# The transposed tokens of the two PEER stages moved by 64 bytes against the weights in on-chip memory

## The chip, the core and the metric

The kernel runs on one core of one Trainium2 chip. Time is device microseconds of one execution, from the median of a few runs. The core has a matrix engine (PE, whose weight loads are shown apart as PEld), a vector engine (DVE), a scalar engine (ACT), a further engine (POOL) and queues for transfers. SBUF is the on-chip memory of 128 partitions. A tile there is a byte range that is the same in every partition, and its address below is the first byte of this range.

## The reference

A trunk of two layers on 256 tokens of 1024 features: a token mixer (attention) in each layer, and after each one a PEER stage, which retrieves experts by product keys. Only the PEER stage is touched:

```python
q = (xc @ w_q).reshape(t, PEER_HEADS, 2, PEER_QDIM // 2)
sc = jnp.einsum('thpc,hpnc->thpn', q, sub_keys)
...                                        # top 16 of each half, then of their sums
u = u_tab[expert]
act = jax.nn.gelu(jnp.einsum('thkd,td->thk', u, xc), approximate=False)
w = (g * act).astype(xc.dtype)
return jnp.einsum('thk,thkd->td', w, v_tab[expert])
```

There are 16384 experts, and `u_tab` and `v_tab` are 16384 x 1024 in float32.

## The kernel before

No expert is gathered. A PEER stage (`peer`) multiplies all tokens with all experts and keeps the chosen ones by a gate matrix. It has three parts, each a long run of matmuls.

- The query projection: 16 blocks of `w_q`, each 8 chunks of 128 features, tokens as the moving operand (256 columns). Here the tokens are the tiles `rhi0..7` and `rlo0..7` of the pool `rawt`.
- The product with the up table: 128 blocks of 128 experts, tokens again the moving operand, now the normalised ones in `hi0..7` and `lo0..7` of the pool `hp`. Its result is `S`, which ScalarE takes through a GELU into `A`, while the gates are made beside it (`gates`, with its own small matmuls on L1011).
- The product with the down table: 128 blocks. The roles turn: the split activations (`ohA`, `ohB`, made by `wsplit` from `A`) are loaded as weights, and rows of the table are the moving operand (512 columns), summed in `acc`.

Every float32 operand is split into a high part of reduced width (`hi`) and the remainder (`lo`), and each product is three matmuls: high by high, and the two mixed ones. In the first two parts that is `split_prod` (L819 to L821): `a` and `b` are 128-column slices of a weight tile's high and low part, which PE loads, and `hi[c]`, `lo[c]` are token tiles of 128 x 256 in 4-byte elements, which PE streams. In the down table it is `mm` (L1099 to L1101).

All weights come through one class (`Weights`): a 512 KB transfer into `raw`, then for each half a ScalarE copy to `hi` (L69) and a VectorE subtraction to `lo` (L70), in five tiles each of 2048 bytes from the pools `hip` and `lop`. The slices loaded by `split_prod` are 512 bytes long.

Where the tiles lie (bytes; the number behind the slash is the address modulo 512, the residue): the weights' `hi` from 40096 / 160 and `lo` from 50336 / 160; `ident` at 24736 / 160; the tokens `hi0` at 172704 / 160, `rhi0` at 199328 / 160; `ohB` from 191136 / 160 and `ohA` from 195232 / 160. As all steps between tiles of a group are multiples of 512, each whole group has its first tile's residue. The filler tile of 192 bytes in `body` (pool `fill`) takes part in these numbers.

Three other places matter for the argument. The first projection (`product`, L301 to L303) has a group of 200-column matmuls in pairs: the second of a pair streams its weights from 800 bytes further on, so from residue 448, while the tokens that it loads stay at 160; the first streams from 160. The transposes of the attention (`transposed`, L400) load slices of the probabilities `P`, which lie at residue 0 in the first layer and at 448 in the second, and stream `ident` from 160 in both. The transposes of L713 load slices of `ks` and `qs` that are 384 bytes apart, so they run through four residues in turn, and stream `ident` too.

Of the kernel before, what the change touches and what calls it, by code (L numbers as in the profile page):

```python
# [9 lines left out]
F32 = mybir.dt.float32  # L10
# [136 lines left out]
def body(tc, I, out):  # L147
    nc = tc.nc
    with ExitStack() as ctx:
# [131 lines left out]
        def tiles8(pool, name, dtype=F32R):  # L281
            return [pool.tile([128, S], dtype, name=f"{name}{c}") for c in range(8)]
# [475 lines left out]
        def peer(layer, gcol, final=False):  # L758
            with ExitStack() as c1:
# [6 lines left out]
                def scr(n):  # L766
                    o = off[0]
                    off[0] += n
                    assert off[0] <= (NA - SCR) * S, off
                    return flat[:, o:o + n]  # L770

                hp = c1.enter_context(tc.tile_pool(name="hp", bufs=1))
# [3 lines left out]
                R1 = hp.tile([128, S // 4, 2, 4], BF, name="R1")  # L776
                RE, RM = hp.tile([128, S], BF, name="RE"), hp.tile([128, 2, S], F16, name="RM")
                RA = hp.tile([128, 3, 4 * len(GA)], F32, name="RA")
                hi, lo = tiles8(hp, "hi"), tiles8(hp, "lo")
                rawc = ExitStack()  # L780
                rawpool = rawc.enter_context(tc.tile_pool(name="rawt", bufs=1))
                scv = scr(2 * 16 * 128)
                sc = scv.rearrange("p (a b c) -> p a b c", a=2, b=16)
                sk = scr(2048).rearrange("p (j n) -> p j n", j=16)
# [82 lines left out]
                def stage2():  # L867
# [85 lines left out]
                    for k, (c, z) in enumerate(((r1T, 1.0), (e2, 1.0), (e2, -1.0))):  # L953
                        nc.scalar.activation(RA[:, k].rearrange("p (g t) -> p g t", t=4),
                                             c.rearrange("p (g t) -> p g t", t=4)[:, GA[0]::AM], AF.Copy, scale=z)
# [5 lines left out]
                def gates():  # L961
                    def hot(t0, E, G):
# [8 lines left out]
                        def pair(i, relu):  # L971
                            if act:
                                for j in (i, i + 1):
                                    r = [RA[:, n, k + j:k + j + 1] for n in range(3)]
                                    if relu:
# [140 lines left out]

        even_mixer(0)
        peer(0, 16)
        mla_mixer(8)
        peer(1, 24, True)  # L1120


# [59 lines left out]
```

## Time and profile before

| what | value |
| --- | --- |
| median of 3 runs | 1887.8 us (1887.28 to 1888.87) |
| the profiled execution | 1887.42 us, of which the span 1885.6 us and 1.8 us around it |
| PE | 1863.1 us busy, 99% of the span |
| PE weight loads | 1687.9 us, 90% |
| VectorE, ScalarE | 1433.7 us (76%), 1248.0 us (66%) |
| bytes read from HBM | 319.97 MB, 170 GB/s over the span |

The span is the time from the first to the last instruction of the profiled execution. Matmuls overlap in a pipeline: the duration of one is its latency, and the pace of the engine is the distance from one start to the next.

### The profile page before, as it was taken

Reading aid. Unit: us, or ns where it says so; the run is one execution under the profiler, and the core shown is the slowest. Engines: PE = TensorE matmul, PEld = TensorE weight load, DVE = VectorE, ACT = ScalarE, POOL = GpSimd, SP = SyncE. Lnnn points to the kernel's source line nnn. Section 1 sums busy time; section 2 is a strip of 40 time slices with the busy share of each in tenths; the row PEclk is TensorE's granted clock in tenths of the full one; section 3 lists DMA queues with packets and bytes.
Section 4 is the critical chain, followed back from the end, with each engine's and each line's share of the span. In section 5 each row is a group of like instructions: output and inputs, shape, how many; then the busy total and the mean of one; then the engine's idle time right before and its main releaser. Section 6 shows DMA issues by size and latency. Waiting matters only on the chain.

```text
span 1885.6 us, 35589 instructions
## 1 busy us (share of the span) xinstructions
PE 1863.1 (99%) x12568; PEld 1687.9 (90%) x12568; DVE 1433.7 (76%) x3586; ACT 1248.0 (66%) x3060; POOL 15.0 (1%) x34
## 2 busy tenths in 40 slices
PE   9999999999999999999999999999999999999998
PEld 7779999999999888888888899999999988888886
DVE  7968998878897666666677699987788976666665
ACT  5656557888876555555577565578888765555554
POOL 0000000000000000000000000000000000000000
PEclk9999999999999999999999999999999999999999
DMA  6434555555455665555553345555555555665664
GB/s 201 124 112 146 185 180 174 167 161 166 158 160 176 192 196 193 192 197 192 184 167 122 124 148 189 183 166 163 161 164 162 168 178 191 193 197 191 193 197 147
DMA packets 90178, 323.33 MB, mean 171 GB/s; under 512 B 10512, under 2 KB 10896, under 8 KB 89744
## 3 DMA queue, kind: packets, MB, share of 16 engines
q1 hardware_dynamic: 88416, 318.18, 52.9%
q8 instruction: 99, 1.62, 0.4%
q0 software_dynamic: 288, 2.10, 0.3%
q10 hardware_dynamic: 1296, 0.78, 0.1%
q14 instruction: 79, 0.65, 0.1%
HBM read 319.97 MB, written 1.05 MB: 170 GB/s over the span
## 4 chain that ended last, share of the span: by engine, by line
PE 95%; DVE 3%; ACT 1%; issue 0%; DMA 0%; POOL 0%; DVEq 0%; POOLq 0%; ACTq 0%
PE S L819 15%; PE S L820 15%; PE S L821 15%; PE acc L1099 12%; PE acc L1101 12%; PE acc L1100 12%; PE scp L1011 3%; PE pj L301 2%; PE pj L303 2%; PE pj L302 2%; DVE lo L70 1%; PE bk L375 1%; PE scp L1048 1%; PE pj L439 1%; PE pj L440 1%; PE pj L441 1%
## 5 line engine op out<-in xcount | busy, mean ns | idle before, releaser
L69 ACT ACTIVATE hi<-raw 128x512 fp32r<-128x512 f32 (+2 forms) x1214 | 756.2, 628 | 567.2 <-PE S L820 191.0
L70 DVE TENSOR_TENSOR lo<-raw,hi 128x512 fp32r<-128x512 f32 (+2 forms) x1214 | 825.8, 685 | 370.8 <-ACT hi L69 362.4
L819 PE MATMUL S<-hi,hi 128*128 128x256 f32 x2048 | 591.0, 289 | 0.5 <-ACT A L1040 0.5
L820 PE MATMUL S<-lo,hi 128*128 128x256 f32 x2048 | 580.6, 284 | 0.0
L821 PE MATMUL S<-hi,lo 128*128 128x256 f32 x2048 | 580.1, 284 | 0.0
L819 PEld LDWEIGHTS S<-hi,hi 128*128 128x128 f32 x2048 | 393.4, 192 | 0.9 <-ACT A L1040 0.9
L820 PEld LDWEIGHTS S<-lo,hi 128*128 128x128 f32 x2048 | 393.8, 192 | 0.0
L821 PEld LDWEIGHTS S<-hi,lo 128*128 128x128 f32 x2048 | 393.0, 192 | 0.0
L1100 PE MATMUL acc<-lo,ohB 128*128 128x512 f32 x512 | 199.5, 390 | 0.0
L1100 PE MATMUL acc<-lo,ohA 128*128 128x512 f32 x512 | 199.5, 390 | 0.0
L1101 PE MATMUL acc<-hi,ohA 128*128 128x512 f32 x512 | 199.2, 390 | 0.0
L1101 PE MATMUL acc<-hi,ohB 128*128 128x512 f32 x512 | 198.5, 390 | 0.0
L1099 PE MATMUL acc<-hi,ohB 128*128 128x512 f32 x512 | 158.5, 390 | 0.0
L1099 PE MATMUL acc<-hi,ohA 128*128 128x512 f32 x512 | 158.2, 390 | 0.0
L976 ACT ACTIVATE ohB<-ohB,RA 128x128 bf16<-128x128 bf16 x256 | 117.2, 525 | 0.0
L1099 PEld LDWEIGHTS acc<-hi,ohA 128*128 128x128 f32 x512 | 96.2, 188 | 19.9
L1100 PEld LDWEIGHTS acc<-lo,ohA 128*128 128x128 f32 x512 | 96.2, 188 | 19.9
L1101 PEld LDWEIGHTS acc<-hi,ohB 128*128 128x128 f32 x512 | 96.2, 188 | 19.9
L1101 PEld LDWEIGHTS acc<-hi,ohA 128*128 128x128 f32 x512 | 96.2, 188 | 19.8
L1099 PEld LDWEIGHTS acc<-hi,ohB 128*128 128x128 f32 x512 | 96.2, 188 | 19.8
L1100 PEld LDWEIGHTS acc<-lo,ohB 128*128 128x128 f32 x512 | 96.1, 188 | 19.9
L1040 ACT ACTIVATE A<-S 128x256 f32<-128x256 f32 (+43 forms) x252 | 76.0, 302 | 13.3 <-PE S L821 13.2
(261 smaller groups left out, 2428.9 us busy)
## 6 DMA issues: line engine op xcount, KB each, us to landing
raw<-in_pu SPq DMA_DIRECT2D x256, 512.0 KB, 3.5
raw<-in_pv SPq DMA_DIRECT2D x256, 512.0 KB, 4.3
raw<-in_pq SPq DMA_DIRECT2D x32, 512.0 KB, 3.5
raw<-in_w SPq DMA_DIRECT2D x20, 512.0 KB, 3.9
raw<-in_uq SPq DMA_DIRECT2D x9, 512.0 KB, 4.1
raw<-in_w SPq DMA_DIRECT2D x12, 352.0 KB, 3.0
raw<-in_w0o SPq DMA_DIRECT2D x8, 512.0 KB, 3.6
raw<-in_w1o SPq DMA_DIRECT2D x8, 512.0 KB, 3.5
```

Of the source, the lines that this page charges most:

```text
L69: self.nc.scalar.activation(hi[:, :w], src, AF.Copy)
L70: self.nc.vector.tensor_tensor(lo[:, :w], src, hi[:, :w].bitcast(F32), op=OP.subtract)
L301: nc.tensor.matmul(ps[tb], hi[c][:, t], a, start=st, stop=False)
L819: nc.tensor.matmul(p, a, hi[c], start=first and i == 0, stop=False)
L820: nc.tensor.matmul(p, a, lo[c], start=False, stop=False)
L821: nc.tensor.matmul(p, b, hi[c], start=False, stop=last and i == 3)
L976: nc.scalar.activation(e[:, j // 2, :, j % 2], e[:, j // 2, :, j % 2], AF.Relu, bias=r[1], scale=r[2])
L1011: nc.tensor.matmul(p[:, i], E[:, 1, i // 2, :, i % 2], G[:, s, i // 2, :, i % 2], start=i + s == 0, stop=True, skip_group_check=True)
L1040: nc.scalar.activation(a[:, T:], p[:, T:], AF.Gelu)
L1099: nc.tensor.matmul(o, a[:, 0, t], w[0], start=b == 0, stop=False)
L1100: nc.tensor.matmul(o, a[:, 0, t], w[1], start=False, stop=False)
L1101: nc.tensor.matmul(o, a[:, 1, t], w[0], start=False, stop=b == NK - 1)
```

## The change

Three tiles that nothing writes or reads are placed between others. `fill0` (448 bytes, that is 64 less than 512) ahead of the tokens `hi`, `lo`; `fill1` (64 bytes) behind them; `fill2` (448 bytes) ahead of `rhi`, `rlo`.

```diff
                 RA = hp.tile([128, 3, 4 * len(GA)], F32, name="RA")
+
+                hp.tile([128, 112], F32, name="fill0")
                 hi, lo = tiles8(hp, "hi"), tiles8(hp, "lo")
+                hp.tile([128, 16], F32, name="fill1")
                 rawc = ExitStack()
                 rawpool = rawc.enter_context(tc.tile_pool(name="rawt", bufs=1))
+                rawpool.tile([128, 112], F32, name="fill2")
```

The addresses that result:

| tiles | before | after |
| --- | --- | --- |
| weights `hi`, `lo`, `A`, `ident`, all of the mixers | unchanged | unchanged |
| tokens `hi0`.. | 172704 / 160 | 173152 / 96 |
| `act`, `ohB`, `ohA` | from 189088 / 160 | from 189600 / 160 |
| raw tokens `rhi0`.. | 199328 / 160 | 200288 / 96 |
| normalised `x` (`xn00`..) | 215712 / 160 | 216672 / 96 |
| `A1` | 199328 / 160 | 199840 / 160 |

No instruction is added, removed or moved: on PE, DVE, ACT, POOL and the transfer queue the programs hold the same instructions in the same order with the same waits (13277, 2999, 2697, 39 and 615 rows). Only operand addresses differ.

## Rows read from the trace of the kernel before

**Rows 1.** The page: span, busy time by engine, granted clock in 40 slices

```profile
span 1885.6 us, 35589 instructions
...
PE 1863.1 (99%) x12568; PEld 1687.9 (90%) x12568; DVE 1433.7 (76%) x3586; ACT 1248.0 (66%) x3060; POOL 15.0 (1%) x34
...
PEclk9999999999999999999999999999999999999999
```

**Rows 2.** The page: the chain that ended last, by engine and line

```profile
PE 95%; DVE 3%; ACT 1%; issue 0%; DMA 0%; POOL 0%; DVEq 0%; POOLq 0%; ACTq 0%
PE S L819 15%; PE S L820 15%; PE S L821 15%; PE acc L1099 12%; PE acc L1101 12%; PE acc L1100 12%; PE scp L1011 3%; PE pj L301 2%; PE pj L303 2%; PE pj L302 2%; DVE lo L70 1%; PE bk L375 1%; PE scp L1048 1%; PE pj L439 1%; PE pj L440 1%; PE pj L441 1%
```

**Rows 3.** The page, costliest groups: shapes, count, busy us, mean ns

```profile
L819 PE MATMUL S<-hi,hi 128*128 128x256 f32 x2048 | 591.0, 289 | 0.5 <-ACT A L1040 0.5
```

**Rows 4.** Groups by shape: the query projection's matmuls

```profile
L819 PE MATMUL S<-rhi,hi 128*128 128x256 f32 x256 | 75.0, 294 | 0.1
```

**Rows 5.** Timeline of PE, up table: start us, us, instruction

```profile
534.32 0.28 PE L821 MATMUL S<-hi,lo 128*128 128x256 f32 x1
...
536.60 0.28 PE L819 MATMUL S<-hi,hi 128*128 128x256 f32 x1
```

**Rows 6.** Timeline of PE, product with the down table

```profile
699.63 0.39 PE L1101 MATMUL acc<-hi,ohB 128*128 128x512 f32 x1
...
705.75 0.62 PE L1099 MATMUL acc<-hi,ohB 128*128 128x512 f32 x2
```

**Rows 7.** Timeline of PE: an S matmul followed by a gate product

```profile
533.44 0.28 PE L821 MATMUL S<-hi,lo 128*128 128x256 f32 x1
533.56 0.64 PE L1011 MATMUL scp<-ohA,ohB 128*128 128x128 f16 x8
```

**Rows 8.** Timeline of PE's weight loads, same place

```profile
533.33 0.19 PEld L821 LDWEIGHTS S<-hi,lo 128*128 128x128 f32 x1
533.56 0.46 PEld L1011 LDWEIGHTS <-ohB 128*128 128x128 bf16 x8
```

**Rows 9.** Instructions of L821: duration ns min/median/max

```profile
L821 PEld LDWEIGHTS S<-hi,lo x2048: 187/192/193, 192.1 to 1527.9; 128*128 128x128 f32 x187
L821 PE MATMUL S<-hi,lo x2048: 278/284/365, 192.2 to 1528.1; 128*128 128x256 f32 x187
```

**Rows 10.** Instructions of L1100, columns as before

```profile
L1100 PEld LDWEIGHTS acc<-lo,ohB x512: 187/188/193, 595.6 to 1873.4; 128*128 128x128 f32 x171
L1100 PE MATMUL acc<-lo,ohB x512: 388/390/398, 595.8 to 1873.6; 128*128 128x512 f32 x171
```

**Rows 11.** Timeline of PE, first projection, matmuls of 200 columns

```profile
16.08 0.28 PE L301 MATMUL pj<-hi,hi 128*128 128x200 f32 x1
...
16.42 0.52 PE L302 MATMUL pj<-lo,hi 128*128 128x200 f32 x2
...
18.13 0.27 PE L301 MATMUL pj<-hi,hi 128*128 128x200 f32 x1
...
18.46 0.52 PE L302 MATMUL pj<-lo,hi 128*128 128x200 f32 x2
```

**Rows 12.** Weight loads of L400, first layer's attention, 60 to 140 us

```profile
L400 PEld LDWEIGHTS bk<-ident,P x32: 137/141/144, 78.1 to 114.6; 128*128 128x128 f32 x32
```

**Rows 13.** The same loads in the second layer's, 1000 to 1080 us

```profile
L400 PEld LDWEIGHTS bk<-ident,P x32: 137/140/144, 1014.0 to 1051.3; 128*128 128x128 f32 x32
```

**Rows 14.** Weight loads of L713 from ks, all

```profile
L713 PEld LDWEIGHTS bk<-ident,ks x32: 122/126/130, 981.4 to 1022.6; 128*96 128x96 f32 x32
```

**Rows 15.** Groups by shape: what writes the tokens of one PEER stage half

```profile
L290 ACT ACTIVATE hi<-acc,gains 128x256 fp32r<-128x256 f32 x16 | 7.5, 471 | 0.0
L291 DVE SCALAR_TENSOR_TENSOR lo<-acc,gains,hi 128x256 fp32r<-128x256 f32 x16 | 7.5, 468 | 0.0
```

**Rows 16.** Busy us by stretch: PE, PEld, DVE, ACT, POOL; PEclk, DMA, GB/s

```profile
190.00:250.00 60.00, 60.00 (x503) 60.00 (x502) 60.00 (x315) 34.55 (x65) 0.00 (x0) 1.00 0.57 182
300.00:400.00 100.00, 100.00 (x913) 99.06 (x912) 77.74 (x187) 84.33 (x255) 0.00 (x0) 1.00 0.52 163
```

## The prediction

> **What bounds the kernel now.** I read the page first. PE is busy for 99% of the span, at a granted clock in the top tenth of all 40 slices [rows 1]: the higher level, 2.4 GHz. The chain that ended last is 95% PE; its lines L819 to L821 carry about 15% each, L1099 to L1101 about 12% each, and VectorE 3% [rows 2]. So what counts is the pace of two kinds of matmul, and other engines matter only where they stop PE.
>
> The pace is read from starts in the timeline, since durations are latencies that overlap. In the product with the up table PE starts 20 matmuls from 534.32 to 536.60 us, 19 steps of 120.0 ns [rows 5]. In the product with the down table 27 steps lie between 699.63 and 705.75 us (between the two rows stand 18 rows of one matmul and 4 of two), 226.7 ns each [rows 6]. The second kind has 256 columns more and takes 106.7 ns more: 2.4 columns per ns, one per cycle. What is left of either is the same 13.3 ns (120.0 - 106.7 and 226.7 - 213.3).
>
> The change touches the first kind alone. Each of its three lines has 2048 instructions in the up product [rows 3] and 256 in the query projection [rows 4], so 3 x 2304 = 6912, and 6912 x 0.120 = 829 us, 44% of the span. One ns per matmul is worth 6.9 us. What a measurement of this kernel can tell from no change is about 0.2%, 3.8 us, so 0.55 ns per matmul.
>
> **The change part by part.** Nothing is added, removed or moved in any queue, so no new wait can be built in, and the sum has one open term: does a pair of reads by PE, the token stream of one matmul and the load of the next one's weights, go at another pace when the streams start 64 bytes apart modulo 512 and not level?
>
> *Is there a price for that pair today?* At 533.44 us an L821 matmul starts, and the next load is not one of 4-byte weights: it begins at 533.56, when this matmul has had its 0.12 us [rows 7, 8]. So here the token stream ran with no load beside it, and the next matmul still came 0.12 us later. The 13.3 ns are thus not mainly the price of a load that is read at the same time. The down product says the same: its loads have long ended when the 213 ns stream does, and the rest is again 13.3 ns. A small price can hide in it. A load beside 256 columns takes 192 ns at the median, one beside 512 columns 188, and the shortest of L821's matmuls takes 278 ns against a median of 284 [rows 9, 10]. So 0 to 4 ns per matmul may be contention: 0 to 28 us.
>
> *Does the offset matter where it differs already?* Three rows tell. In the first projection, matmuls of 200 columns stream from residue 448 at 16.08 to 16.42 us and from 160 at 18.13 to 18.46, beside loads from 160 in both; three steps take 0.34 and 0.33 us, so 113 and 110 ns, apart by the rounding of the view [rows 11]. The loads of L400 take 141 ns from residue 0 and 140 from 448, exactly 64 bytes apart, against a stream from 160 [rows 12, 13]. Those of L713 run through four residues and lie between 122 and 130 ns [rows 14]. No row shows a price of the offset. But all these paces are set by the loads, about 110 ns for 128 columns: a 200-column stream needs 83.3 + 13.3 = 96.7 ns, and up to 13 ns of delay to it would be hidden. For S matmuls, whose own stream sets the pace, no row has another offset. So the term lies between -4 ns, all of the contention seen, and +13 ns, all that the 200-column rows could hide: -28 to +90 us. I take 0, since the nearest rows, with 64 bytes and with 288 bytes of difference, show none.
>
> The Trainium skill ("SBUF — State Buffer", section "Who interferes with whom") gives PE two read ports of its own, one for the moving operand and one for weight loads. By that rule the term is 0 at any offset; the 4 ns between 192 and 188 [rows 9, 10] are no proof against it, since such a load is also followed sooner by the next.
>
> The other edits cost nothing. The fillers have no instruction. The 32 ScalarE and 32 VectorE instructions that write a token tile (half of them in the form shown) take 0.47 us each [rows 15], and lie beside PE's stream; they keep their shapes. The split activations, `act` and `A1` move by 512 bytes and keep their residue, so the down product stays at 226.7 ns.
>
> The sum: 1885.6 us of span + 6912 x 0 + 1.8 us around it = 1887.4 us, 0.4 us under the median of the runs shown. I forecast **1887.5 us**; this case by itself lies within 1884 to 1891.
>
> **The rivals.**
>
> *The small contention goes away (faster).* Tokens are read at 2.4 x 4 = 9.6 bytes per ns, and weights at 512 bytes in about 110 ns, 4.7 bytes per ns, from [rows 5, 6, 11]. Level at the start, the stream is a full 512 bytes ahead of the load after some 104 ns, so both are at the same residue again just as they end. With 64 bytes less it gets that far only after about 118 ns, when the load is over. If the 4 ns are this meeting, up to 4 ns go. For it: the 192 ns of the loads in this stage alone, and a shortest matmul of 278 ns. Against it: the 200-column rows and L400 show no trace of an offset. At 3 ns, between the ends but nearer to what the rows show, 6912 x 3 = 21 us: **1867 us**. In the 190 to 250 us stretch VectorE is busy for all 60 us, in 300 to 400 for 78 [rows 16], so that a small part would not arrive.
>
> *A new meeting near the start (slower).* Level, the faster stream leads from its first byte. From 64 bytes behind it catches up with the load 64 / (9.6 - 4.7) = 13 ns after the start and must pass it. If two reads at one residue get in each other's way, this adds a meeting that the present layout has not. Price: 64 bytes of the stream, 6.7 ns, or 6912 x 6.7 = 46 us: **1934 us**; at the bound of 13 ns, 1977 us. It decides from 0.55 ns on. For it: no row of a stream-bound pair excludes it. Against it: the streams of 448 against loads of 160 start 288 bytes off, must also meet once, and keep 110 ns.
>
> *The 13.3 ns go altogether (much faster).* They could belong to where a stream starts and not to its pair. With 120.0 replaced by the 110 ns at which loads follow each other [rows 11], the floor, 10 x 6912 = 69 us: **1818 us**. Against it: the lone L821 [rows 7, 8] has them, and both kinds of matmul, from different pools, have them equally.
>
> The Trainium skill ("TensorE: Matmul & The Clock Gate", section "Back-to-back issue gap") states a spacing of N / 2.4 + 2.5 ns, thus 109 ns for 256 columns, where the rows show 120. By that figure alone 11 ns per matmul, an estimate of 75 us, would be there to win; the trace does not bear the figure out for any of these 4-byte matmuls.
>
> **How the numbers follow.** No change 0.42, since every row with an offset shows none; the small gain 0.30, since the rows leave 4 ns open; the large gain 0.05; the meeting at the start, up to about 7 ns, 0.16; the same from 7 to 13 ns 0.07. That makes faster 0.35, same 0.42, slower 0.23. The range runs from 1864 us, just under the small gain, to 1934 us, the middle price of the loss. Outside are the large gain, the upper part of the loss, and some of the small gain, near 0.15 together.
>
> **What the changed profile would show.** If I am right: 120.0 ns between starts of L823 to L825 (the same lines, four further down), 226.7 ns between those of the down product, medians of 284 and 192 ns, shares of the chain as before. If the small gain is right: starts 116 to 119 ns apart, loads of 188 ns. If the meeting is right: 121 to 133 ns, durations longer by the same amount, in both layers, and nothing else changed; VectorE and ScalarE would then be idle for longer. A change in the down product's 226.7 ns would refute that residues of the unmoved pairs stay what they were. I am wrong if PE is sensitive to an offset in a pair that its stream bounds, which no row here tests.

## The result, and the profile after

The changed kernel takes 1872.31 us (median of 4 runs, 1871.02 to 1874.3); the kernel before 1888.34 us (1887.28 to 1890.65). The ratio is 0.9915, with a 95% interval of 0.9899 to 0.9931: 16 us or 0.85% faster. The profiled execution took 1871.02 us. A fifth execution of one of the runs below, e7, the profiled one, took 3716.78 us where the other four took 1870.5 to 1874.15; its time and its rows are not used. The page of the changed kernel answers to [rows 1] and [rows 2]:

```profile
span 1869.2 us, 35589 instructions
...
PE 1845.6 (99%) x12568; PEld 1668.6 (89%) x12568; DVE 1431.8 (77%) x3586; ACT 1245.3 (67%) x3060; POOL 15.0 (1%) x34
...
PEclk9999999999999999999999999999999999999999
...
PE 93%; DVE 4%; ACT 1%; issue 1%; DMA 0%; POOL 0%; DVEq 0%; POOLq 0%; ACTq 0%
PE S L823 14%; PE S L825 14%; PE S L824 14%; PE acc L1103 12%; PE acc L1104 12%; PE acc L1105 12%; PE scp L1015 3%; PE pj L301 2%; PE pj L303 2%; PE pj L302 2%; DVE lo L70 1%; PE bk L375 1%; PE scp L1052 1%; PE pj L439 1%; PE pj L440 1%
```

The span is 16.4 us shorter, PE is still busy for 99% of it, and the granted clock is the same. VectorE's share of the chain rises from 3 to 4%. The S lines have 14% each where they had 15%; the acc lines stay at 12%.

The instructions of one S line and of one acc line of the changed kernel (duration ns min/median/max), against [rows 9] and [rows 10]:

```profile
L825 PEld LDWEIGHTS S<-hi,lo x2048: 186/188/192, 191.5 to 1511.6; 128*128 128x128 f32 x187
L825 PE MATMUL S<-hi,lo x2048: 276/281/394, 191.6 to 1511.7; 128*128 128x256 f32 x187
```

```profile
L1104 PEld LDWEIGHTS acc<-lo,ohB x512: 187/188/193, 587.9 to 1857.0; 128*128 128x128 f32 x171
L1104 PE MATMUL acc<-lo,ohB x512: 389/389/395, 588.1 to 1857.2; 128*128 128x512 f32 x171
```

In S the medians of the loads went from 192 to 188 ns and those of the matmuls from 284 to 281. In acc the loads stayed at 188 ns and the matmuls at 389 to 390. The timeline of PE in the changed kernel's down product (start us, duration us, instruction) gives the same as [rows 6]:

```profile
699.90 0.39 PE L1104 MATMUL acc<-lo,ohA 128*128 128x512 f32 x1
...
705.34 0.39 PE L1104 MATMUL acc<-lo,ohA 128*128 128x512 f32 x1
```

There are 24 steps between these rows, of 226.7 ns each. The up product, against [rows 5], in a stretch where PE stops once:

```profile
249.79 0.28 PE L823 MATMUL S<-hi,hi 128*128 128x256 f32 x1
...
251.80 0.28 PE L825 MATMUL S<-hi,lo 128*128 128x256 f32 x1
252.39 0.39 PE L823 MATMUL S<-hi,hi 128*128 128x256 f32 x1 [0.31 <-ACT A L1044]
252.62 0.28 PE L824 MATMUL S<-lo,hi 128*128 128x256 f32 x1
...
255.91 0.28 PE L823 MATMUL S<-hi,hi 128*128 128x256 f32 x1
```

Ahead of the stop 17 steps take 2.01 us, 118 ns each; behind it 29 steps take 3.29 us, 113.4 ns each. So the new layout does not have one pace but two, where the old one had 120 throughout. Over all 6521 pairs of S matmuls that start directly one after the other, the mean step is 117.09 ns (before, over 6531: 119.87): 16% lie at 113 or 114, mean 113.3, and nearly all others at 117 to 119, mean 117.8. A run keeps its pace until PE has stopped or has done other matmuls.

The account closes. The steps won 6521 x 2.78 = 18.1 us; the time between consecutive S starts with PE's stops in it fell from 822.9 to 806.4 us, a difference of 16.5 us, so 1.6 us went back into stops; and the span fell by 16.4 us. The windows of the changed kernel (busy us and instructions of PE, PEld, DVE, ACT, POOL, then granted clock, DMA share, GB/s) show where it was lost:

```profile
190.00:250.00 60.00, 59.78 (x506) 59.19 (x505) 60.00 (x315) 34.53 (x68) 0.00 (x0) 1.00 0.56 183
...
300.00:400.00 100.00, 100.00 (x932) 99.02 (x931) 80.34 (x196) 85.57 (x262) 0.00 (x0) 1.00 0.51 162
```

From 300 to 400 us PE does 932 matmuls where it did 913; from 190 to 250 us, where VectorE is busy for all 60 us, only 506 where it did 503 [rows 16].

### The profile page after: what moved, and what is told of

Same layout as the page of the kernel before. It is cut to its first block, busy times and chain, and to the rows that moved or that the text cites. A ratio compares the mean times of both kernels' runs of the same rounds, so it can differ in the third digit from the quotient of the medians.

```text
span 1869.2 us, 35589 instructions
## 1 busy us (share of the span) xinstructions
PE 1845.6 (99%) x12568; PEld 1668.6 (89%) x12568; DVE 1431.8 (77%) x3586; ACT 1245.3 (67%) x3060; POOL 15.0 (1%) x34
## 4 chain that ended last, share of the span: by engine, by line
PE 93%; DVE 4%; ACT 1%; issue 1%; DMA 0%; POOL 0%; DVEq 0%; POOLq 0%; ACTq 0%
PE S L823 14%; PE S L825 14%; PE S L824 14%; PE acc L1103 12%; PE acc L1104 12%; PE acc L1105 12%; PE scp L1015 3%; PE pj L301 2%; PE pj L303 2%; PE pj L302 2%; DVE lo L70 1%; PE bk L375 1%; PE scp L1052 1%; PE pj L439 1%; PE pj L440 1%
## 5 line engine op out<-in xcount | busy, mean ns | idle before, releaser
L823 PE MATMUL S<-hi,hi 128*128 128x256 f32 x2048 | 584.9, 286 | 0.6 <-ACT A L1044 0.6
L824 PE MATMUL S<-lo,hi 128*128 128x256 f32 x2048 | 574.4, 281 | 0.0
L825 PEld LDWEIGHTS S<-hi,lo 128*128 128x128 f32 x2048 | 387.2, 189 | 1.7 <-DVE lo L70 1.7
L824 PEld LDWEIGHTS S<-lo,hi 128*128 128x128 f32 x2048 | 388.6, 190 | 0.0
L823 PEld LDWEIGHTS S<-hi,hi 128*128 128x128 f32 x2048 | 385.1, 188 | 1.1 <-ACT A L1044 1.0
L980 ACT ACTIVATE ohB<-ohB,RA 128x128 bf16<-128x128 bf16 x256 | 117.4, 527 | 0.0
L982 ACT ACTIVATE ohB<-iota,RA 128x128 bf16<-128x128 f32 x256 | 84.2, 436 | 0.0
```

The lines of the kernel that those rows point to most:

```text
L823: nc.tensor.matmul(p, a, hi[c], start=first and i == 0, stop=False)
L824: nc.tensor.matmul(p, a, lo[c], start=False, stop=False)
L825: nc.tensor.matmul(p, b, hi[c], start=False, stop=last and i == 3)
L980: nc.scalar.activation(e[:, j // 2, :, j % 2], e[:, j // 2, :, j % 2], AF.Relu, bias=r[1], scale=r[2])
L982: nc.scalar.activation(e[:, j // 2, :, j % 2], iota, AF.Square, bias=r[0], scale=-1.0)
```

## The experiments

All edits are against the kernel before, and change addresses alone; every kernel computes the whole of the reference. "Offset" is the residue of the token stream less that of the weights that are loaded, in the S product: 0 before, -64 in the changed kernel. The table has every run; the step is the mean distance of consecutive S starts, "fast" the share of steps of at most 115 ns, acc the step in the down product. Only at an offset of 64, or 192, are such steps runs of 113 and 114 ns; at 32 and 128 they are single steps of 115 ns or less in a mixed cycle (with 128: about 120, 119, 115, 118, 122). The kernel before, run again beside them, took 1889.27 us (first four), 1889.07 us (next four), 1887.93 us (next three) and 1888.03 us (last).

| run | offset | us | ratio (95%) | S step ns | fast | acc ns |
| --- | --- | --- | --- | --- | --- | --- |
| before | 0 | 1888.34 | 1 | 119.87 | 0% | 226.7 |
| after | -64 | 1872.31 | 0.9915 (0.9899 to 0.9931) | 117.09 | 16% | 226.7 |
| e1_below32 | -32 | 1880.04 | 0.9953 (0.9937 to 0.997) | 118.30 | 4% | 226.7 |
| e2_below128 | -128 | 1884.12 | 0.9975 (0.9965 to 0.9986) | 119.02 | 13% | 226.7 |
| e3_below256 | -256 | 1888.79 | 0.9998 (0.9989 to 1.0008) | 119.89 | 0% | 226.7 |
| e4_above64 | +64 | 1870.35 | 0.9899 (0.9883 to 0.9916) | 116.86 | 21% | 226.7 |
| e5_activations_too | -64 | 1867.28 | 0.9885 (0.9869 to 0.9902) | 115.09 | 61% | 228.9 |
| e6_above192 | +192 | 1871.96 | 0.9913 (0.9896 to 0.9929) | 116.93 | 20% | 226.7 |
| e7_normalised_only | -64 | 1872.68 | 0.9915 (0.9898 to 0.9931) | | | |
| e8_above96 | +96 | 1887.92 | 0.9996 (0.9986 to 1.0006) | 119.83 | 2% | 226.7 |
| e9_gates_below_split_level | -64 | 1860.4 | 0.9848 (0.9831 to 0.9864) | 114.79 | 68% | 226.7 |
| e10_weights_above64 | -64 | 1866.08 | 0.9888 (0.9871 to 0.9904) | 114.89 | 66% | 228.9 |
| e11_all_above64 | +64 | 1897.37 | 1.0051 (1.0034 to 1.0067) | 117.69 | 2% | 233.3 |
| e12_gates_tiles_alone | -64 | 1859.33 | 0.9852 (0.9835 to 0.9868) | 114.98 | 63% | 226.7 |

### e4_above64: the other sign

```diff
+                hp.tile([128, 16], F32, name="fill0")
                 hi, lo = tiles8(hp, "hi"), tiles8(hp, "lo")
+                hp.tile([128, 112], F32, name="fill1")
...
+                rawpool.tile([128, 16], F32, name="fill2")
```

> Tokens 64 bytes above the weights' residue. A: the stream is 512 bytes ahead after 91 ns, well inside the load, so no gain: 1888 us or more, loads of 192 ns. B: 1872 us, as with 64 bytes below. C: not tied to the sign either way.

It took 1870.35 us, as fast as 64 below or a little faster. By the meeting at the end of the stream, which 64 bytes less are to avoid, 64 bytes more had to leave it in. That mechanism is refuted; at 64 bytes the tokens gain with either sign. One S line of this kernel (duration ns min/median/max):

```profile
L824 PEld LDWEIGHTS S<-hi,lo x2048: 186/188/193, 191.6 to 1510.0; 128*128 128x128 f32 x187
L824 PE MATMUL S<-hi,lo x2048: 276/279/393, 191.8 to 1510.1; 128*128 128x256 f32 x187
```

### e1_below32, e2_below128, e3_below256: the size

The same three lines with other lengths:

```diff
# e1_below32
+                hp.tile([128, 120], F32, name="fill0")
+                hp.tile([128, 8], F32, name="fill1")
+                rawpool.tile([128, 120], F32, name="fill2")
# e2_below128
+                hp.tile([128, 96], F32, name="fill0")
+                hp.tile([128, 32], F32, name="fill1")
+                rawpool.tile([128, 96], F32, name="fill2")
# e3_below256
+                hp.tile([128, 64], F32, name="fill0")
+                hp.tile([128, 64], F32, name="fill1")
+                rawpool.tile([128, 64], F32, name="fill2")
```

> Tokens 32 bytes below the weights' residue. Theory A (a meeting at the end of the load, where the stream is a whole 512 bytes ahead; passing the load early costs nothing): with 32 bytes the meeting falls at about 111 ns, the end of the load, so between 1872 and 1888 us, S starts 118 to 120 ns apart. Theory B (both reads begin at the same residue and disturb each other there; any difference frees them): as with 64 bytes, 1872 us within 4. Theory C (the pace depends on the exact offset by a lock between stream and load): any of 113, 118 or 120 ns, so 1845 to 1888 us.

> Tokens 128 bytes below. A: the meeting at the end is gone, the passing after 26 ns is free: 1872 us within 4, starts 118 ns apart. B: 1872 us. C: may go back to 1888 us or down to 1845 us (113 ns).

> Tokens 256 bytes below (or above, modulo 512). A: passing after 52 ns, in the middle of the load, and no meeting at the end: 1872 us. B: 1872 us. If a passing in mid-load costs anything: above 1888 us. C: anything from 1845 to 1900 us.

32 bytes give about half of the gain, 128 between a quarter and a third, and 256 none at all: the step is 119.89 ns, and the loads are back at 192 ns, as the S line of that kernel shows:

```profile
L824 PEld LDWEIGHTS S<-hi,lo x2048: 187/192/192, 194.3 to 1530.2; 128*128 128x128 f32 x187
L824 PE MATMUL S<-hi,lo x2048: 278/283/364, 194.4 to 1530.3; 128*128 128x256 f32 x187
```

So it is not the distance in bytes that helps, and not any difference either (theory B); 256 counts like 0.

### e6_above192: is 256 the period?

```diff
+                hp.tile([128, 48], F32, name="fill0")
+                hp.tile([128, 80], F32, name="fill1")
+                rawpool.tile([128, 48], F32, name="fill2")
```

> Tokens 192 bytes above, which is 64 below modulo 256. Theory C1 (what counts is the offset modulo 256, in which 256 is no offset at all): as with 64 bytes either way, 1871 us within 4, starts 117 ns apart in the mean. Theory C2 (what counts is the distance from the residue modulo 512, and the gain is gone with distance): between 128 and 256 bytes, 1886 us within 3.

1871.96 us, the time of 64 below. With e3 this shows, at the two offsets tried, that they count modulo 256 here: +192 is -64.

### e8_above96: is more than 64 better?

```diff
+                hp.tile([128, 24], F32, name="fill0")
+                hp.tile([128, 104], F32, name="fill1")
+                rawpool.tile([128, 24], F32, name="fill2")
```

> Tokens 96 bytes above. C1 and C2 both: between 64 bytes (1870 us) and 128 bytes (1884 us), 1877 us within 4. If the pace were a matter of a few single offsets, it could be at 1888 us or under 1865 us.

The expectation of a time between those of 64 and 128 missed: 96 gives nothing (1887.92 us), though its loads take 187 ns at the median. The timeline of PE of this kernel:

```profile
399.76 0.28 PE L823 MATMUL S<-lo,hi 128*128 128x256 f32 x1
...
401.92 0.28 PE L823 MATMUL S<-lo,hi 128*128 128x256 f32 x1
```

18 steps take 2.16 us, 120.0 ns, as before; but they are not equal. In the trace's own nanoseconds they repeat a cycle of about 116, 125, 116, 123, 119 and 121. A shorter load thus does not by itself bring a faster pace, and the gain does not rise steadily with the offset.

### e7_normalised_only: which of the two products

```diff
+                hp.tile([128, 112], F32, name="fill0")
                 hi, lo = tiles8(hp, "hi"), tiles8(hp, "lo")
+                hp.tile([128, 16], F32, name="fill1")
```

> Only the normalised tokens of the up product lie 64 bytes below; the raw tokens of the query projection are back at the weights' residue. If the gain is one per matmul, 6144 of 6912 of it stays, 14 of 16 us: 1874 us, and the query projection's starts are 120 ns apart again. If the query projection had most of it: nearer to 1888 us.

Only the up product's tokens move; the query projection's stay level. 1870.5 to 1874.15 us in four executions, the changed kernel's time: what the projection's 768 of 6912 matmuls add is within the spread. Rows that tell the two products apart are in the changed kernel's trace: there the projection's mean step fell from 119.5 to 116.0 ns, and the up product's from 119.9 to 117.2, so both gain, and 768 x 3.5 = 2.7 us is the projection's part.

### e5_activations_too: the split activations move with the tokens

```diff
+                hp.tile([128, 112], F32, name="fill0")
```

> Split activations lie 64 bytes below as well, so that in the down product the stream begins 64 bytes above the load. Theory P (the price belongs to stream and load that take equally long, as in the S matmuls): the down product stays at 226.7 ns and the time at 1872 us within 4. Theory Q (every pair at one residue pays, the down product's 13.3 ns are of the same kind): up to 6.7 ns less for 3072 matmuls, 1852 us. A loss in the down product would show above 1876 us.

Without `fill1`, `act`, `ohA`, `ohB` and `A1` lie 64 bytes lower too. Faster than the changed kernel by 5 us, which no change of the S pairs explains, since these are the same. Theories P and Q both missed: neither has the down product slower. The acc step is worse, 228.9 for 226.7 ns (3072 x 2.2 = 6.8 us), but S gains more: 61% of its steps are fast, not 16%. By the account, 793.9 - 822.9 + 6.8 = -22.2 us; the span is 1864.6 us, 21.0 less than before.

### e9_gates_below_split_level, e12_gates_tiles_alone: what sets the share of fast steps

In the kernels with an offset of 64 a run of S matmuls keeps its pace, but for a handful of changes in the midst of a run, and can change it behind the gates' matmuls (`scp`), which load and stream the one-hot tiles of the pool `ohp`. Theory L: those tiles' residue decides at which pace S goes on. e9 is e5 with the split activations put back at 160; e12 is the changed kernel with, modulo 512, nothing but the gates' one-hot tiles 64 bytes lower.

```diff
# e9_gates_below_split_level (with e5's filler)
-                        return [ohp.tile([128, 4, 128], F32, name=n).rearrange("p t i -> p (t i)").bitcast(d).rearrange(
+                        return [ohp.tile([128, 640], F32, name=n)[:, :512].bitcast(d).rearrange(
...
-                    t = ohp.tile([128, 4, 128], F32, name="ohA" if b % 2 else "ohB").rearrange("p (s h) e -> p s (h e)", s=2).bitcast(F32R)
+                    t = ohp.tile([128, 640], F32, name="ohA" if b % 2 else "ohB")[:, 16:528].rearrange("p (s e) -> p s e", s=2).bitcast(F32R)
# e12_gates_tiles_alone: the same, and back at residue 160:
-                        t = ohp.tile([128, S], F32, name="act")
+                        t = ohp.tile([128, 384], F32, name="act")[:, 16:272]
...
-                    q = ohp.tile([128, S], F32, name="act")
+                    q = ohp.tile([128, 384], F32, name="act")[:, 16:272]
...
+                pa.tile([128, 16], F32, name="fill3")
```

> As the run with the split activations 64 bytes below too, but these alone are put back to the weights' residue (their tiles get 512 bytes more, and they start 64 bytes in); the gates' one-hot tiles, which use the same buffers earlier, stay 64 bytes below. Theory L (which pace an S run locks to is decided where it starts again behind the gates' matmuls, by the gates' tiles' residue; the down product depends on its own pair): S starts 115 ns apart as there, the down product back at 226.7 ns: 1867 - 3069 x 2.2 ns = 1860 us within 3. Rival (the share of fast runs came from another tile or by chance): S at 117 ns, 1872 us.

> Of the tiles behind the tokens only the gates' one-hot tiles stay 64 bytes below; the GELU outputs, the queries, the last blocks of A and the split activations are back at the weights' residue. Against the changed kernel it differs in these one-hot tiles alone. Theory L (an S run locks where it starts again behind the gates' matmuls, and these tiles' residue decides to which pace): about two thirds of the starts 113 ns apart, 1860 us within 3. Rival (one of the other tiles decided it): a sixth, as in the changed kernel, 1872 us.

Both come out as theory L forecast: 1860.4 and 1859.33 us, with 68% and 63% of the steps fast and acc at 226.7 ns. They are the fastest versions, 1.5% under the kernel before. Both also have larger tiles in `ohp`; e5, with the old sizes and the gates' tiles 64 below too, has 61% of fast steps, so the size is not needed. PE's timeline in e12, around a group of gate matmuls:

```profile
509.30 0.28 PE L822 MATMUL S<-hi,lo 128*128 128x256 f32 x1
...
511.00 0.28 PE L822 MATMUL S<-hi,lo 128*128 128x256 f32 x1
511.12 0.63 PE L1012 MATMUL scp<-ohA,ohB 128*128 128x128 f16 x8
511.56 0.36 PE L820 MATMUL S<-hi,hi 128*128 128x256 f32 x1
511.76 0.28 PE L821 MATMUL S<-lo,hi 128*128 128x256 f32 x1
511.88 0.28 PE L822 MATMUL S<-hi,lo 128*128 128x256 f32 x1
...
513.13 0.28 PE L821 MATMUL S<-lo,hi 128*128 128x256 f32 x1
```

Two such places in the changed kernel, the first behind steps of 113 ns, the second behind steps of 118:

```profile
506.73 0.28 PE L823 MATMUL S<-hi,hi 128*128 128x256 f32 x1
...
508.99 0.28 PE L825 MATMUL S<-hi,lo 128*128 128x256 f32 x1
509.11 0.63 PE L1015 MATMUL scp<-ohA,ohB 128*128 128x128 f16 x8
...
509.75 0.28 PE L824 MATMUL S<-lo,hi 128*128 128x256 f32 x1
...
511.28 0.28 PE L825 MATMUL S<-hi,lo 128*128 128x256 f32 x1
...
520.60 0.64 PE L1015 MATMUL scp<-ohA,ohB 128*128 128x128 f16 x8
521.04 0.36 PE L823 MATMUL S<-hi,hi 128*128 128x256 f32 x1
521.24 0.28 PE L824 MATMUL S<-lo,hi 128*128 128x256 f32 x1
...
523.95 0.28 PE L823 MATMUL S<-hi,hi 128*128 128x256 f32 x1
```

In e12 the steps take 113 ns ahead of the gates (15 in 1.70 us) and 114 behind them (11 in 1.25 us, from 511.88). In the changed kernel 20 steps of 113 ns (2.26 us) come ahead of the first place and 13 of 118 ns (1.53 us) behind it; from 521.24 us 23 take 2.71 us, 118 each. Each kernel has 124 places with a group of eight gate matmuls. S goes on at the fast pace, at most five steps later, behind 106 of them in e12, in e9 and in e5, behind 10 in the changed kernel, and behind 40 in e4.

What the residue changes is narrower than theory L has it: it decides whether the 113 ns outlive the gates. In e12, S had 113 ns ahead of 102 of the places and kept them behind all 102; of the 22 places with 118 ns ahead, 18 had 118 behind too. In the changed kernel the 113 ns were kept at none of 14 places, in e4 at none of 38, while 118 ns turned into 113 at 10 of 110 and 40 of 86. Where most places have 113 ns behind them, PE does more matmuls in the window from 300 to 400 us, 951 in e12:

```profile
300.00:400.00 100.00, 100.00 (x951) 99.15 (x950) 81.35 (x199) 86.92 (x266) 0.00 (x0) 1.00 0.52 168
```

### e10_weights_above64: the weights move, not the tokens

```diff
+        ctx.enter_context(tc.tile_pool(name="fillw", bufs=1)).tile([128, 16], F32, name="fillw")
...
-        ctx.enter_context(tc.tile_pool(name="fill", bufs=1)).tile([128, 48], F32, name="fill")
+        ctx.enter_context(tc.tile_pool(name="fill", bufs=1)).tile([128, 32], F32, name="fill")
```

> The weights' high and low tiles lie 64 bytes higher instead, all tokens and activations unmoved. If only the difference between stream and load counts: S as in the run where everything else lies 64 bytes below, 115 ns, the down product 229 ns, about 1868 us. If the tokens' own address counts (or their distance from other tiles): S at 120 ns and 1889 us or more.

The tokens stay where they were; the weights, and with them the pairs of the mixers, shift. S steps of 114.89 ns: it is the difference that counts, not the place of either. The down table's rows are such weights too, and stream 64 above the split activations that are loaded: 228.9 ns, as in e5.

### e11_all_above64: e5 with the other sign

```diff
+                hp.tile([128, 16], F32, name="fill0")
```

> Tokens and split activations (and the gates' tiles) 64 bytes above the weights. S as with tokens 64 bytes above or better, 115 to 117 ns; the down product's stream now begins 64 bytes below its loads. If the sign doesn't count there either: 229 ns, 1867 us. If it does: 226.7 ns or less, 1860 us or less.

1897.37 us, slower than before; both expected times missed. S keeps most of its gain (117.69 ns), though with 2% of fast steps: gate tiles 64 above the weights do not do what 64 below does. But the down product, whose stream now lies 64 below its loads, loses more than that. Its timeline:

```profile
704.86 0.39 PE L1101 MATMUL acc<-lo,ohA 128*128 128x512 f32 x1
...
710.46 0.39 PE L1101 MATMUL acc<-lo,ohA 128*128 128x512 f32 x1
```

24 steps take 5.60 us, 233.3 ns each. That is 6.7 ns more in each of 3072, 20.4 us; with the 13.0 us that S gains (822.9 to 809.9) the sum is +7.4 us, and the span is 8.1 us longer.

## Why the prediction failed in its likeliest case

**What holds.** PE's pace was the bound: the span moved by what the S matmuls' starts moved. The down product stayed at 226.7 ns, as the unmoved pairs were to. The fillers cost nothing: in e3 and e8, where the pace is that of before, so is the time. Where VectorE is busy throughout, from 190 to 250 us, the gain hardly arrived, as said.

**The step that failed** is "the 13.3 ns are thus not mainly the price of a load that is read at the same time", drawn from [rows 7, 8], and the choice of 0 that followed. An S matmul that is followed by a load for the gates stays within 3 ns of the pace of its run. In the trace's nanoseconds that load begins 117.4 ns after it before (132 cases); in the changed kernel 113.3 in the 18 cases whose run is fast and 118.8 in the other 114; in e12 113.2 (106 cases) and 118.1 (26). So what a lone matmul takes depends on the run that it ends, and says nothing on what another offset does. Nor is it without a load beside it: [rows 8] have the load for this same matmul from 533.33 us for 0.19 us, so 0.08 us into its stream. At the fast pace 113.3 - 106.7 = 6.6 ns of the 13.3 are left: half of them did hang on the layout.

**The rows with other offsets** [rows 11 to 14] could not see it. The prediction said that their loads hide up to 13 ns, and still took them for the nearest; and three steps that are read to 0.01 us give one step to some 3 ns, as much as was won. The term is -2.8 ns (119.87 to 117.09), within the bounds of -4 and +13 that it gave; only the choice within them was wrong. Times 6912 it is 19 us, of which 16 arrived.

**The small gain** had the price (3 ns, measured 2.8), the time (1867 us, measured 1872) and the signs right, starts at 116 to 119 ns and loads at 188, but not the mechanism; that the time fell into the range is owed to this rival, and that its price came out is luck. e4 refutes the meeting at the end, and e8 refutes that the 4 ns of the loads are what is won: its loads have 187 ns and its pace is that of before.

**The large gain** did not come: the shortest mean step of any run is 114.79 ns (e9). Nor does its cause hold, the place where a stream starts: in e10 the tokens did not move, and S gained as in e5.

**The slower meeting at the start** does not show in S, which gains at 64 bytes of either sign. For 512-column streams a loss of the size that was priced, 6.7 ns, does occur in e11, with the stream 64 below, and 2.2 ns with it 64 above (e5, e10); that it is that meeting is not shown.

**The rule on read ports** of the Trainium skill ("SBUF — State Buffer", section "Who interferes with whom"), by which the term is 0 at any offset, does not agree with these runs on that zero: with nothing but operand addresses changed, the S step lies between 114.8 and 119.9 ns, the acc step between 226.7 and 233.3. That PE's two reads disturb each other is not shown by this.

**What is shown and what stays open.** Shown: the offset of stream and load, not the place of either (e10), sets S's pace, with 256 as 0 and 192 as -64 (e3, e6); both signs of 64 gain (e4); the pace is then one of two, is kept over a run, and the residue of the gates' tiles decides whether the fast one is kept across them (e9, e12). Not settled: what first sets a run to the fast pace, what PE or the memory does in the two, why 96 bytes give nothing and 128 little, and why the down product is best when level while S is worst.

## What to carry to other kernels

Where a run of matmuls with 4-byte operands is bound by its own stream, the addresses of the streamed and the loaded tile modulo 256 are worth a sweep of a few fillers: 64 either way gave 0.85 to 1% here, and with the small matmuls' tiles in between moved too, but the down product's left level, 1.5%. Sweep each kind of product by itself, since what helps 256 columns cost the 512-column product up to 3%. And a row whose pace is set by something else, or a lone instruction inside a steady run, is no evidence that an effect is absent.

## What the runs showed of the hardware

- The mean step of a 256-column matmul of 4-byte operands was 119.87 ns level, 118.30 with the stream 32 bytes below the load, 119.83 with it 96 above, 119.02 with it 128 below and 119.89 with it 256 below; at 64 either way it was 117.8 or 113.3.
- In the changed kernel a run stays at 113.3 or at 117.8 ns over tens to hundreds of matmuls; all 108 changes between them lie within the first five steps behind a stop of PE or behind other matmuls.
- The pace of 113 ns outlived a group of eight gate matmuls in 102 of 102 cases with the gates' tiles 64 bytes below the weights (e12), and in 0 of 14 with them level (the changed kernel).
- The step of a 512-column matmul was 226.7 ns level, 228.9 with the stream 64 bytes above the load and 233.3 with it 64 below.
